# Partial products collected from two PSUM banks at a time, branch gating over all tokens in one step, and one modulation buffer in two merges of a two-layer diffusion backbone

## The chip, the cores and the metric

The kernel runs on one core of a Trainium2 chip as one program. The metric is device time in microseconds, the median of several runs. PE is TensorE, DVE is VectorE, ACT is ScalarE, POOL is GpSimd, and SP is the engine that issues all DMAs here.

## The reference, cut to what matters

Two layers work on 512 latent and 256 context tokens of width 1024. The second layer computes outputs for the latent tokens only.

```python
h = rms_norm(x, g_pre) * (1 + scale) + shift              # scale, shift, gate from silu(c) @ w_mod
z = h @ w_in                                              # 11 pieces of 512 columns, and 3 x 1024 merge logits
o_ret  = rms_norm(retention(rq, rk, rv)) * silu(rg)       # branch r
o_mlp  = mu * (w_s @ layer_norm(mv) + b_s) * silu(mg)     # branch m
o_diff = rms_norm(diff_attention(dq, dk, dv)) * silu(dg)  # branch d
y   = sum over b in r, m, d of sigmoid(logits_b) * (o_b @ w_bo[b])
out = x + gate * rms_norm(y @ w_o, g_post)
```

## The kernel before, in words

**Numbers.** Every large matmul is made of three: weights and activations are split into a high part in fp32r (a copy on ACT, line 341) and a low part (a subtraction on DVE, line 353), and high x high, high x low and low x high are summed in PSUM.

**Blocks.** Weights come as named blocks of 256 output columns. `dl`, `rl`, `ml` are the merge logits of the branches d, r and m, four blocks each; `db`, `rb`, `mb` are the branch output weights, four each; `rg`, `mg`, `mu`, `dg`, `mv` are the gates and inputs of the branches, two each. A block is loaded into `raw[0]` or `raw[1]`, two buffers of 2048 words a partition that take turns, `mg0` into `raw[0]` and `mg1` into `raw[1]`. From there it is split into slots in the fp32r area `AR`.

**Seven products.** Where the table `SEVEN` names a block (`dl`, `rl`, `ml`, `mg`, `mu` in both layers, `rg` in the first), `seven` (line 1581) computes a 2 x 2 block product with seven instead of eight half-size products, after Strassen and Winograd. A product is 12 matmuls over n = 384 tokens in layer 0 and n = 256 in layer 1, into a PSUM bank of its own. It is added to running sums: one copy on ACT, then seven adds on DVE, each of one product. A finished quarter goes to `done`, which takes its sigmoid on ACT, and the like. The weights of a product are one of seven pieces that `p_split` makes, up to five pieces ahead (`NSLOT`); four more DVE instructions form the pieces' sums.

**Merges.** `merge` (line 1705) runs for d, r and m in turn. For each of four blocks it computes the sigmoids of the logits, then the branch products for two groups of 128 channels, span by span (two spans of 384 tokens in layer 0, one of 512 in layer 1). Each span's product is gated by one DVE multiplication and added to `Y`, by POOL in merge r and DVE in merge m.

**Modulation.** While layer 0's merges run, DVE also computes the modulation vectors that are needed later. `mod_begin` (line 1047) sets up buffers of 1024 words in `AF`: n for the rows of `w_mod`, n = 2, and two for the silu of the two conditioning rows. `mod_load` brings in a part of `w_mod` (512 KB), and `mod_item` sums its product with each of the two conditioning rows, one custom DVE instruction each (line 376), whose elementwise result is junk and goes to the upper half of `raw[1]`. That half is free as long as the blocks alternate between 2048 and 1024 words, which they do in a merge. Merge d takes eight such loads, merges r and m twelve each, a few behind each group of channels (`MODS`).

**Order.** The functions only record operations, in program order, with the memory that they read and write. `Rec.schedule` (line 406) then list-schedules them: it steps through time with an estimated cost for each operation and puts on each engine the ready operation of the lowest priority number, which is the program order plus a bump by kind. The result is emitted as one fixed order an engine. So a change in one stage can move instructions in later ones. In the attention stage of a layer (`dr_phase`) units of differential attention (`d_unit`: scores, softmax, transposes, product with V) and of retention are interleaved on PE with projections in groups of 24 matmuls, which take turns in two PSUM banks.

Of the kernel before, what the change touches and what calls it, by code (L numbers as in the profile page):

```python
# [200 lines left out]
class Rec:  # L201
# [14 lines left out]
    def iv(self, ap):  # L216
        pat = ap.ap
        t = ap.tensor
        sp = str(ap.space)
        if "DRAM" in sp.upper() or type(t).__name__ == "DRamTensorHandle":  # L220
            ext = 1 + sum((n - 1) * s for s, n in pat)
            return "D" + t.name, [(ap.offset, ap.offset + ext)], None
        ps = pat[0][0]
        f = ap.offset % ps
        p0 = ap.offset // ps
        outer, ln = [], 1
        dims = [d for d in pat[1:] if d[0] != 0 and d[1] > 1]
        while dims:
            s, n = dims[-1]
            if s == ln or (ln == 1 and s <= 2):  # L230
                ln = (n - 1) * s + ln
                dims.pop()
            else:
                break
        starts = [f]
        for s, n in dims:
            starts = [x + s * k for x in starts for k in range(n)]
        return t.name, [(x, x + ln) for x in starts], range(p0 // 32, (p0 + pat[0][1] - 1) // 32 + 1)
# [346 lines left out]
class Prog:  # L585
# [995 lines left out]
    def seven(self, l, name, done):  # L1581

        R, F = self.R, self.F
        n = self.half(l)
        tag = R.tag = f"L{l}.{name}"
        S1, S2, S3, S4 = (self.SX[j] for j in range(4))

        def p(x, A):
            wh, wl = self.pw[self.ahead(l, name, x)]
            R.tag = tag  # L1590
            ps = self.P(n)
            with R.pe():
# [8 lines left out]
        def add(out, ps, f):
            R.tt(out.ap, ps.ap, f.ap, ALU.add)

        def give(m, t, c):
            done(m, n * t, n * t + n, c.ap)
            c.free()
# [12 lines left out]
        ps.free()
        p5 = p(3, S1)  # L1620
        c12 = F(n)
        add(c12, p5, u)
        ps = p(4, S3)
        add(u, ps, u)
        ps.free()
        c = F(n)
        add(c, p5, u)
        p5.free()
        give(1, 1, c)
        ps = p(5, self.halves(1, 1))  # L1630
        add(u, ps, u)
        ps.free()
        give(0, 1, u)
        ps = p(6, S4)
        add(c12, ps, c12)
        ps.free()
        give(1, 0, c12)
# [67 lines left out]
    def merge(self, l, c, extra=None):  # L1705
# [7 lines left out]
                self.fm.take(o, o + n)  # L1713
                self.Y.append(Buf(self.fm, self.AFl, o, n, (n,)))
        for p in range(4):
            G = {}

            def done(m, a, b, ps):
                if m not in G:
                    G[m] = F(n)  # L1720
# [12 lines left out]
            if SEVEN[l]:  # L1733
                q = self.ahead(l, name)
                W = [[x[:, k] for x in self.pw[q + e]] for e in range(2) for k in range(2)]
            else:
                self.begin(l, name)
                hi, lo = self.W(l, name, 256, 0, 4)
                W = [(hi[:, k], lo[:, k]) for k in range(4)]
            for m in range(2):  # L1740
                i = 2 * p + m
                y = self.Y[i]
                for v, a, b in self.spans(l) if l == 0 or not end else ((0, 0, 256), (1, 256, 512)):
                    R.tag = f"L{l}.{name}"
                    pb = self.P(b - a)
                    with R.pe():
                        for k in range(4):
                            wh, wl = (x[:, 128 * m:128 * m + 128] for x in W[k])
                            xh, xl = (x[:, k, a:b] for x in self.OT)
                            R.mm(pb.ap, wh, xh, k == 0, False)  # L1750
                            R.mm(pb.ap, wh, xl, False, False)
                            R.mm(pb.ap, wl, xh, False, k == 3)
                    R.tag += ".ev"
                    g = G[m][:, a:b]
                    R.tt(y[:, a:b] if first else g, pb.ap, g, ALU.mult)
                    pb.free()
# [274 lines left out]
    def run(self):  # L2031
# [4 lines left out]
        for l in range(DEPTH):  # L2036
# [125 lines left out]
```

## Time and profile before

| | |
|---|---|
| runs | 1476.3, 1476.57, 1474.8 us; median 1476.3 |
| profiled execution | 1477.75 us, of which the span of instructions 1476.0 |
| granted TensorE clock | 0.999 of full speed |
| attention stages | about 63 to 376 us (layer 0), 866 to 1138 (layer 1) |
| merges d, r and m, layer 0 | about 402 to 502, 522 to 625, 679 to 786 |
| gMLP stage (`mg`, `mu`), layer 0; layer 1 | about 614 to 692; 1308 to 1370 |
| DVE instructions | 2119, busy 1086.6 us |

Rows of the profile name line, engine, operation and the tiles that it writes and reads: `AR` is the fp32r area, `AF` the float area, `PSM` is PSUM. `x12` counts instructions; times are us unless marked ns. A `<-` behind an idle time names what ended it.

### The profile page before, as it was taken

The numbers are of one execution on the slowest core, as the hardware profiler recorded it, in microseconds if no ns is written. First come the engines' busy times: TensorE is split into PE (matmuls) and PEld (weight loads), VectorE is DVE, ScalarE is ACT, GpSimd is POOL, SyncE is SP. The second block draws the span as 40 slices with busy tenths as digits, with TensorE's granted clock in tenths as the row PEclk, the third lists the DMA queues.
The fourth block names the chain that finished last, engine by engine and source line by source line (L and its number), as shares of the span: only waits on it lengthen the run. The fifth ranks groups of instructions, "written<-read, shape, count | busy, mean of one in ns | idle before, by whom it ended". The sixth has DMA issues, their size and how long they took to land.

```text
span 1476.0 us, 24501 instructions
## 1 busy us (share of the span) xinstructions
PE 1448.1 (98%) x9424; PEld 1354.4 (92%) x9424; DVE 1086.6 (74%) x2119; ACT 689.6 (47%) x1488; POOL 173.6 (12%) x195
## 2 busy tenths in 40 slices
PE   6999999999999999999999999999999999999998
PEld 4789898999999999999999898989898998999997
DVE  4456655557998799999996645674858786899982
ACT  6735653564343343344346443564455354444551
POOL 1211211211000002211001111111111000111000
PEclk9999999999999999999999999999999999999999
DMA  9351322112223334322364234141212222322332
GB/s 362 124 162 58 88 69 68 37 63 81 91 103 129 108 107 145 127 78 103 120 228 147 73 127 131 63 122 44 86 51 81 70 101 106 129 94 87 142 129 72
DMA packets 38869, 159.00 MB, mean 108 GB/s; under 512 B 5472, under 2 KB 6624, under 8 KB 29280
## 3 DMA queue, kind: packets, MB, share of 16 engines
q1 hardware_dynamic: 38752, 157.43, 31.4%
q8 instruction: 74, 1.21, 0.3%
q14 instruction: 43, 0.35, 0.1%
HBM read 135.39 MB, written 6.82 MB: 96 GB/s over the span
## 4 chain that ended last, share of the span: by engine, by line
PE 83%; DVE 9%; issue 3%; DMA 2%; ACT 2%; POOL 1%; SPq 1%; DVEq 0%; POOLq 0%; ACTq 0%
PE PSM L316 79%; DVE AR L353 3%; DVE AF L353 3%; PE PSM L320 3%; DMA AF<-w 1%; POOL AF L394 1%; ACT AF L341 1%; DVE AF L372 1%; SPq L403 1%; ACT AR L341 1%; DMA AF<-x 0%; DVE AF L362 0%; DVE AF L368 0%; DVE AF L376 0%; DVE AF L360 0%
## 5 line engine op out<-in xcount | busy, mean ns | idle before, releaser
L316 PE MATMUL PSM<-AR 128*128 128x256 f32 (+2 forms) x7896 | 1305.4, 324 | 4.6 <-DVE AF L353 3.9
L316 PEld LDWEIGHTS PSM<-AR 128*128 128x128 f32 x7896 | 1190.8, 190 | 76.6 <-ACT AF L341 3.8
L341 ACT ACTIVATE AR<-AF 128x512 fp32r<-128x512 f32 (+5 forms) x623 | 356.6, 601 | 340.7 <-PE PSM L316 174.6
L353 DVE TENSOR_TENSOR AR<-AF,AR 128x512 fp32r<-128x512 f32 (+4 forms) x620 | 407.5, 681 | 72.3 <-ACT AR L341 67.1
L353 DVE TENSOR_TENSOR AF<-PSM,AF 128x384 f32<-128x384 f32 (+3 forms) x461 | 237.2, 530 | 126.7 <-PE PSM L316 66.9
L394 POOL TENSOR_TENSOR AF<-AF 128x128 f32<-128x128 f32 (+7 forms) x188 | 172.9, 932 | 1297.4 <-DVE AF L353 452.5
L341 ACT ACTIVATE AF<-PSM 128x256 f32<-128x256 f32 (+5 forms) x321 | 137.5, 448 | 201.4 <-PE PSM L316 170.4
L353 DVE TENSOR_TENSOR AF<-AF 128x512 f32<-128x512 f32 (+6 forms) x268 | 160.5, 622 | 15.5 <-PE PSM L316 4.2
L341 ACT ACTIVATE AF<-AF 128x256 f32<-128x256 f32 (+5 forms) x227 | 110.2, 512 | 122.0 <-DVE AF L353 104.4
L316 PE MATMUL PSM<-AF 128*128 128x128 f32 (+3 forms) x1104 | 142.8, 304 | 11.8 <-DMA AF<-wmodn 9.1
L316 PEld LDWEIGHTS PSM<-AF 128*128 128x128 f32 (+1 forms) x1104 | 126.4, 185 | 21.3 <-DVE AF L376 9.1
L341 ACT ACTIVATE AF<-PSM,AF 128x768 f32<-128x768 f32 (+2 forms) x144 | 90.8, 646 | 88.6 <-DVE AF L360 53.1
L372 DVE TENSOR_REDUCE AF<-PSM 128x2 f32<-128x1536 f32 (+1 forms) x40 | 61.6, 1542 | 34.2 <-PE PSM L316 33.9
L362 DVE TENSOR_SCALAR AF<-AF 128x1 f32<-128x1 f32 (+3 forms) x188 | 42.7, 237 | 49.4 <-ACT AF L341 42.9
L320 PE MATMUL PSM<-AF 128*128 128x128 f32 x424 | 68.1, 278 | 5.3 <-ACT AF L341 4.1
L376 DVE CUSTOM_DVE_ANT_0 AF<-AF 128x1024 f32<-128x1024 f32 (+1 forms) x60 | 72.8, 1213 | 0.0
L320 PEld LDWEIGHTS PSM<-AF 128*128 128x128 f32 x424 | 50.8, 142 | 17.3 <-ACT AF L341 7.3
L368 DVE SCALAR_TENSOR_TENSOR AF<-AF 128x768 f32<-128x768 f32 (+2 forms) x48 | 44.2, 928 | 3.6 <-POOL AF L394 2.7
L353 DVE TENSOR_TENSOR AF<-AF,AR 128x512 f32<-128x512 f32 (+2 forms) x40 | 29.8, 766 | 0.6 <-PE PSM L316 0.5
L368 DVE SCALAR_TENSOR_TENSOR AF<-AF,PSM 128x128 f32<-128x128 f32 x64 | 20.5, 344 | 10.8 <-PE PSM L316 5.5
L362 DVE TENSOR_SCALAR AF<-PSM,AF 128x128 f32<-128x128 f32 x48 | 15.8, 402 | 12.7 <-PE PSM L320 12.7
L360 DVE TENSOR_SCALAR AF<-AF 128x2 f32<-128x2 f32 (+5 forms) x98 | 21.4, 235 | 2.1 <-ACT AF L341 0.7
(22 smaller groups left out, 103.9 us busy)
## 6 DMA issues: line engine op xcount, KB each, us to landing
AF<-w SPq DMA_DIRECT2D x74, 1024.0 KB, 4.9
AF<-wmod SPq DMA_DIRECT2D x32, 512.0 KB, 3.5
AF<-w SPq DMA_DIRECT2D x26, 512.0 KB, 4.4
AF<-wmodn SPq DMA_DIRECT2D x16, 512.0 KB, 8.9
AF<-x SPq DMA_DIRECT2D x12, 512.0 KB, 4.3
AR<-AR SPq DMA_DIRECT2D x16, 384.0 KB, 4.2
AF<-AF SPq DMA_DIRECT2D x64, 64.0 KB, 2.0
AF<-const SPq DMA_DIRECT2D x4, 512.0 KB, 3.6
```

Source lines behind the costliest of these rows:

```text
L316: self.add("PE", lambda: pe.matmul(out, lhsT, rhs, start=start, stop=stop), [out], [lhsT, rhs], c)
L320: self.add("PE", lambda: pe.transpose(out, in_, ident), [out], [in_, ident], 109.0)
L341: return self.add("ACT", lambda: e.activation(out, in_, func, **kw), outs, ins, c, tab)
L353: return self.add("DVE", lambda: v.tensor_tensor(out, a, b, op=op), [out], [a, b], self.n(out) / 0.97 + 84)
L360: f = lambda: v.tensor_scalar(out, a, s1, None, op0=op0)
L362: f = lambda: v.tensor_scalar(out, a, s1, s2, op0=op0, op1=op1)
L368: return self.add("DVE", lambda: v.scalar_tensor_tensor(out, a, s, b, op0=op0, op1=op1), [out], ins, self.n(out) / 0.97 + 130)
L372: return self.add("DVE", lambda: v.tensor_reduce(out, in_, axis=AX.X, op=op), [out], [in_], self.n(in_) / 0.96 + 72)
L376: return self.add("DVE", lambda: v.tensor_tensor_reduce(junk, a, b, 1.0, 0.0, ALU.mult, ALU.add, accum), [junk, accum], [a, b], self.n(a) ...
L394: return self.add("POOL", lambda: g.tensor_tensor(out, a, b, op=op), [out], [a, b], c)
L403: return self.add("SP", lambda: e.dma_start(out=out, in_=in_), [out], [in_], 475 if "DRAM" in str(in_.space).upper() else 650, nbytes=nb)
```

## The change

`seven` allocates two banks for a pair of products and adds both with one DVE instruction of 2n elements; the seven adds become four. Banks are released when a pair is done, and the finished quarters are handed on in pairs. In `merge` the branch products of both spans go into one two-bank tile and are gated by one multiplication, followed by one add into `Y`, except in the last block of merge m; the sigmoid buffers are allocated up front. `mod_begin` gets n = 1 for the merges d and r: one buffer for parts of `w_mod`, placed so that the area shrinks by 1024 words. A line in the bookkeeping of intervals treats short accesses with stride two exactly.

```diff
-            if s == ln or (ln == 1 and s <= 2):
+            if s == ln or (ln == 1 and s <= 2 and n > 16):
...
-        self.modb = self.At(7680, n + 2, DM)
+        self.modb = self.At(3584 + 1024 * (n + 2), n + 2, DM)
...
+        def two(x, A, y, B):
+            ps = self.P(2, 512)
+            p(x, A, ps[:, 0, 0:n])
+            p(y, B, ps[:, 1, 0:n])
             return ps
...
-        u = F(n)
-        ps = p(0, self.halves(0, 0))
-        R.copy_a(u.ap, ps.ap)
+        e = F(2, n)
+        u = e[:, 0]
+        ps = self.P(n)
+        p(0, self.halves(0, 0), ps.ap)
+        R.copy_a(u, ps.ap)
         ps.free()
-        c = F(n)
-        ps = p(1, self.halves(0, 1))
-        add(c, ps, u)
+
+        ps = two(1, self.halves(0, 1), 2, S2)
+        d = F(2, n)
+        R.tt(d.ap, ps[:, :, 0:n], u.unsqueeze(1).to_broadcast([128, 2, n]), ALU.add)
         ps.free()
-        give(0, 0, c)
...
+        done(0, 0, n, d[:, 0])
+
+        ps = two(3, S1, 4, S3)
+        R.tt(e.ap, ps[:, :, 0:n], d[:, 1:2].to_broadcast([128, 2, n]), ALU.add)
+        R.tt(d[:, 1], ps[:, 0, 0:n], e[:, 1], ALU.add)
         ps.free()
+        done(1, n, 2 * n, d[:, 1])
+        d.free()
+
+        ps = self.P(2, 512)
+        p(5, self.halves(1, 1), ps[:, 1, 0:n])
+        p(6, S4, ps[:, 0, 0:n])
+        R.tt(e.ap, ps[:, :, 0:n], e.ap, ALU.add)
         ps.free()
+        done(0, n, 2 * n, e[:, 1])
+        done(1, 0, n, e[:, 0])
+        e.free()
...
+                pb = self.P(len(cuts), 512)
+                for v, a, b in cuts:
...
+                            R.mm(pb[:, v, 0:h], wh, xh, k == 0, False)
+                            R.mm(pb[:, v, 0:h], wh, xl, False, False)
+                            R.mm(pb[:, v, 0:h], wl, xh, False, k == 3)
+                R.tag += ".ev"
+
+                for v0, v1 in [(v, v + 1) for v in range(len(cuts))] if end else [(0, len(cuts))]:
+                    cols = slice(h * v0, h * v1)
+                    g = G[m][:, cols]
+                    yc = y[:, cols]
+                    w = lambda x: x.rearrange("p (a b) -> p a b", b=h)
+                    R.tt(w(yc if first else g), pb[:, v0:v1, 0:h], w(g), ALU.mult)
...
-                self.mod_begin()
+                self.mod_begin(1)
             self.merge(l, "d", lambda i: extra(i, MODS[0][i]))
```

**What moves, first place.** SP's order from the end of merge r into the gMLP stage of layer 0. `wmod` is a modulation load, `w 128x2048` and `w 128x1024` are weight blocks. Before, the block of 1024 words is `rb3`, and the `w 128x2048 x2` are `mg0` and `mg1`:

```order
L403 DMA AF<-w 128x1024
L403 DMA AF<-wmod 128x1024 x2
L403 DMA AF<-w 128x2048 x2
L403 DMA AF<-wst 128x512
L403 DMA AF<-bs 128x512
```

In the changed kernel, from `rb3` too; the single `w 128x2048` is `mg0`, and the `x4` are `mu0`, `mg1`, `mu1` and `ml0`:

```order
L403 DMA AF<-w 128x1024
L403 DMA AF<-wmod 128x1024 x2
L403 DMA AF<-wst 128x512
L403 DMA AF<-wmod 128x1024
L403 DMA AF<-w 128x2048
L403 DMA AF<-bs 128x512
L403 DMA AF<-wmod 128x1024 x3
L403 DMA AF<-w 128x2048 x4
```

Three modulation loads and `mu0`'s load have moved ahead of `mg1`'s.

DVE's order at the same place. `L376 ISA AF<-AF 128x1024` is a modulation sum. Before, the two are those over the last load of merge r; the `AR` row behind the first belongs to `rb3`, the one behind the second is `mg0`'s first subtraction:

```order
L376 ISA AF<-AF 128x1024
L376 ISA AF 128x1
L353 TENSOR_TENSOR AR<-AF,AR 128x512
L353 TENSOR_TENSOR AF<-PSM,AF 128x384
L376 ISA AF<-AF 128x1024
L376 ISA AF 128x1
L353 TENSOR_TENSOR AR<-AF,AR 128x512
L353 TENSOR_TENSOR AF<-PSM,AF 128x384
L353 TENSOR_TENSOR AF<-AF 128x4x128
```

In the changed kernel, from the add over the 4th and 5th product of `mg0` (`128x768`); the sum behind it is the last one over the last load of merge r, and the `AR` row is `mg1`'s first subtraction:

```order
L353 TENSOR_TENSOR AF<-PSM,AF 128x768
L376 ISA AF<-AF 128x1024
L376 ISA AF 128x1
L353 TENSOR_TENSOR AF<-PSM,AF 128x384
L353 TENSOR_TENSOR AF<-AF 128x2x2
L360 TENSOR_SCALAR AF<-AF 128x2
L353 TENSOR_TENSOR AF<-AF 128x384
L353 TENSOR_TENSOR AF<-PSM,AF 128x768
L353 TENSOR_TENSOR AF<-AF 128x384 x2
L353 TENSOR_TENSOR AF<-PSM,AF 128x384 x2
L353 TENSOR_TENSOR AR<-AF,AR 128x512 x2
```

The last sum has moved from ahead of `mg0` to behind its 5th product. The two `PSM,AF 128x384` ahead of the `AR` row belong to six matmuls of 128x128 that PE now takes between `mg0`'s seventh product and `mg1`'s first.

**Second place.** PE's order near the end of layer 1's attention stage. `128x512 x2, 128x256 x4, 128x512 x2` are the scores of one attention unit, `L320 x6` its transposes, `L316 AF 128x128 x6` its product with V, and `128x256 x24` a group of projection matmuls. Before, from the scores of the third unit of head 3 (the `x8` holds two transposes of a retention unit and six of the second unit, the `x7` the third unit's six and one more):

```order
L316 MATMUL PSM<-AR 128x512 x2
L316 MATMUL PSM<-AR 128x256 x4
L316 MATMUL PSM<-AR 128x512 x2
L320 MATMUL PSM<-AF 128x128 x8
L316 MATMUL PSM<-AR 128x256 x24
L320 MATMUL PSM<-AF 128x128
L316 MATMUL PSM<-AF 128x128 x6
L316 MATMUL PSM<-AR 128x256 x24
L320 MATMUL PSM<-AF 128x128 x7
```

In the changed kernel, from the same scores to the next projections:

```order
L316 MATMUL PSM<-AR 128x512 x2
L316 MATMUL PSM<-AR 128x256 x4
L316 MATMUL PSM<-AR 128x512 x2
L316 MATMUL PSM<-AF 128x128 x6
L316 MATMUL PSM<-AR 128x512 x2
L316 MATMUL PSM<-AR 128x256 x2
L320 MATMUL PSM<-AF 128x128
L316 MATMUL PSM<-AR 128x256 x2
L316 MATMUL PSM<-AR 128x512 x2
L320 MATMUL PSM<-AF 128x128 x6
L316 MATMUL PSM<-AR 128x256 x24
```

Two groups of projections stood between the third unit's scores and its transposes; now the fourth unit's scores stand there, and the projections come behind. ACT's order there, in the changed kernel: `PSM,AF 128x768` are the third unit's two exponentials, and the `128x256` behind them is the copy that empties the projections' PSUM bank:

```order
L341 ACTIVATE AF<-PSM,AF 128x768
L341 ACTIVATE AF<-PSM,AF 128x128
L341 ACTIVATE AF<-PSM,AF 128x768
L341 ACTIVATE AF<-PSM 128x128
L341 ACTIVATE AF<-PSM 128x256
L341 ACTIVATE AF<-PSM 128x768
```

That copy is the one that the next group of 24 waits for.

More of the change, by code (lines that the diff above doesn't have):

```diff
@@ L1586, in seven, with p @@
         S1, S2, S3, S4 = (self.SX[j] for j in range(4))
-        def p(x, A):
+        def p(x, A, ps):
             wh, wl = self.pw[self.ahead(l, name, x)]
             R.tag = tag
-            ps = self.P(n)
             with R.pe():
@@ L1594, in p @@
                     a, b = A[0][:, k], A[1][:, k]
-                    R.mm(ps.ap, wh[:, k], a, k == 0, False)
-                    R.mm(ps.ap, wh[:, k], b, False, False)
-                    R.mm(ps.ap, wl[:, k], a, False, k == 3)
+                    R.mm(ps, wh[:, k], a, k == 0, False)
+                    R.mm(ps, wh[:, k], b, False, False)
+                    R.mm(ps, wl[:, k], a, False, k == 3)
             R.tag += ".ev"
-            return ps
[L1601 to L1606, printed above, removed]
-        u = F(n)
-        ps = p(0, self.halves(0, 0))
-        R.copy_a(u.ap, ps.ap)
+        def two(x, A, y, B):
+            ps = self.P(2, 512)
+            p(x, A, ps[:, 0, 0:n])
+            p(y, B, ps[:, 1, 0:n])
+            return ps
+        e = F(2, n)
[3 more added lines that the diff above has]
+        R.copy_a(u, ps.ap)
         ps.free()
-        c = F(n)
-        ps = p(1, self.halves(0, 1))
-        add(c, ps, u)
+        ps = two(1, self.halves(0, 1), 2, S2)
+        d = F(2, n)
+        R.tt(d.ap, ps[:, :, 0:n], u.unsqueeze(1).to_broadcast([128, 2, n]), ALU.add)
         ps.free()
-        give(0, 0, c)
-        ps = p(2, S2)
-        add(u, ps, u)
+        done(0, 0, n, d[:, 0])
+        ps = two(3, S1, 4, S3)
+        R.tt(e.ap, ps[:, :, 0:n], d[:, 1:2].to_broadcast([128, 2, n]), ALU.add)
+        R.tt(d[:, 1], ps[:, 0, 0:n], e[:, 1], ALU.add)
         ps.free()
[L1620 to L1624, printed above, removed]
-        ps.free()
[L1626 to L1637, printed above, removed]
+        done(1, n, 2 * n, d[:, 1])
[4 more added lines that the diff above has]
+        R.tt(e.ap, ps[:, :, 0:n], e.ap, ALU.add)
+        ps.free()
+        done(0, n, 2 * n, e[:, 1])
+        done(1, 0, n, e[:, 0])
+        e.free()
     def eight(self, l, name, done):
@@ L1715, in merge @@
         for p in range(4):
-            G = {}
+            G = [F(n), F(n)]
             def done(m, a, b, ps):
-                if m not in G:
-                    G[m] = F(n)
                 R.act(G[m][:, a:b], ps, AF.Sigmoid)
@@ L1742, in merge @@
                 y = self.Y[i]
-                for v, a, b in self.spans(l) if l == 0 or not end else ((0, 0, 256), (1, 256, 512)):
+                cuts = self.spans(l) if l == 0 or not end else ((0, 0, 256), (1, 256, 512))
+                h = cuts[0][2]
+                pb = self.P(len(cuts), 512)
+                for v, a, b in cuts:
                     R.tag = f"L{l}.{name}"
-                    pb = self.P(b - a)
                     with R.pe():
@@ L1749, in merge @@
                             xh, xl = (x[:, k, a:b] for x in self.OT)
[L1750 to L1756, printed above, removed]
+                            R.mm(pb[:, v, 0:h], wh, xh, k == 0, False)
[8 more added lines that the diff above has]
+                    R.tt(w(yc if first else g), pb[:, v0:v1, 0:h], w(g), ALU.mult)
                     if last:
-                        R.tt(y[:, a:b], y[:, a:b], g, ALU.add)
+                        R.tt(yc, yc, g, ALU.add)
                     elif not first:
-                        R.ptt(y[:, a:b], y[:, a:b], g, ALU.add)
+                        R.ptt(yc, yc, g, ALU.add)
+                pb.free()
                 G[m].free()
```

## Prediction

> **What bounds the kernel now.** I read the page's busy shares first, then the list of waits, then PE's timeline, then windows cut at the stages that the change touches.
>
> ```profile
> span 1476.0 us, 24501 instructions
> PE 1448.1 (98%) x9424; PEld 1354.4 (92%) x9424; DVE 1086.6 (74%) x2119; ACT 689.6 (47%) x1488; POOL 173.6 (12%) x195
> PE PSM L316 <- DMA AF<-wmodn: 9.1, 1, 9.1
> PE PSM L316 <- DVE AF L353: 4.2, 7, 1.1
> PE PSM L320 <- ACT AF L341: 4.1, 6, 1.1
> ```
>
> PE (TensorE) works 98% of the span. 9.1 us of its idle time is the first load. All else that it waits for in 1476 us is some 12 us, and only 4.2 us of that is for DVE (VectorE), the engine that the change relieves. So fewer DVE instructions can return only a few us, while each new hole in PE's row is paid in full. Where are the 4.2 us?
>
> ```profile
> 522.00:614.00 92.00, 91.76 (x530) 91.44 (x529) 91.45 (x158) 34.45 (x63) 18.27 (x12) 1.00 0.36 125
> 614.00:680.00 66.00, 66.00 (x399) 66.00 (x398) 62.21 (x109) 27.67 (x49) 12.26 (x8) 1.00 0.23 80
> 1308.00:1338.00 30.00, 30.00 (x238) 29.30 (x237) 29.57 (x55) 14.63 (x31) 3.51 (x3) 1.00 0.24 90
> 1338.00:1368.00 30.00, 26.75 (x216) 25.85 (x216) 30.00 (x61) 13.50 (x28) 5.49 (x4) 1.00 0.28 102
> 1436.00:1476.00 40.00, 33.79 (x175) 28.89 (x174) 11.76 (x26) 5.08 (x16) 2.22 (x4) 0.95 0.20 66
> ```
>
> The columns are the stretch and its length, then busy time of PE, PEld, DVE, ACT and POOL, the granted clock, and DMA. In layer 0's merge r (522 to 614) DVE works 91.45 of 92 us, yet PE loses only 0.24; in its gMLP stage (614 to 680) PE loses nothing. In layer 1's gMLP stage (1308 to 1368) DVE works 59.57 of 60 us and PE idles 3.25. There alone does DVE set the time.
>
> **DVE's saving.** The change removes 130 DVE instructions: 3 in each of 34 seven-product blocks, 28 in layer 0's merges. Element counts stay. DVE in that stage:
>
> ```profile
> 1351.41 0.68 DVE L353 TENSOR_TENSOR AR<-AF,AR 128x512 fp32r<-128x512 f32 x1
> ...
> 1352.02 0.41 DVE L353 TENSOR_TENSOR AF<-AF 128x256 f32<-128x256 f32 x1
> 1352.35 0.41 DVE L353 TENSOR_TENSOR AF<-PSM,AF 128x256 f32<-128x256 f32 x1
> 1352.69 1.35 DVE L353 TENSOR_TENSOR AR<-AF,AR 128x256 fp32r<-128x256 f32 x3
> ```
>
> An add of 512 holds DVE for 0.61 us (1351.41 to 1352.02), one of 256 for 0.33 to 0.34. Two of 256 made one save 0.07, so a block saves 3 x 0.07 = 0.2 us. Four such blocks and the start of a fifth lie in 1308 to 1368: 1.0 us less DVE work where DVE is the bound, so PE's 3.25 us fall by **1.0**. Bounds: 0, if the pairs are collected later by as much, and 3.25, if the new order also spreads the rest; I take 1.0 because no row shows more being removed. [...] Elsewhere PE hides DVE, and the saving is worth 0.2 us at most (layer 0, merge r).
>
> What the pairs add stays hidden. A pair holds two PSUM banks from its first product until its add; with eight banks PE can be three pairs, six products, ahead of an add that takes about 1 us. A merge's product over both token halves comes one branch product later, and its result is read a whole merge later. POOL, 12% busy, makes one add of 768 where it made two of 384. Should a pair be collected so late that PE meets a full PSUM, each such case costs at most one add, 1 us; it is in the bounds of the saving. The line in the interval bookkeeping leaves the order as it was, by itself.
>
> **The single modulation buffer.** This part removes nothing from DVE; it moves work. Each load, the two conditioning rows' as well, has to wait until the previous one is used up.
>
> ```profile
> AF<-w SPq DMA_DIRECT2D x74, 1024.0 KB, 4.9
> AF<-wmod SPq DMA_DIRECT2D x32, 512.0 KB, 3.5
> L376 DVE CUSTOM_DVE_ANT_0 AF<-AF 128x1024 f32<-128x1024 f32 x56 | 71.9, 1284 | 0.0
> L353 DVE TENSOR_TENSOR AF<-PSM,AF 128x256 f32<-128x256 f32 x158 | 64.3, 420 | 48.9 <-ACT AF L341 25.0 <-PE PSM L316 20.0 <-POOL AF L394 1.6
> L353 DVE TENSOR_TENSOR AF<-PSM,AF 128x384 f32<-128x384 f32 x190 | 101.4, 551 | 20.3 <-PE PSM L316 15.0 <-ACT AF L341 4.3
> L353 DVE TENSOR_TENSOR AF<-PSM,AF 128x512 f32<-128x512 f32 x105 | 70.6, 686 | 52.0 <-PE PSM L316 26.4 <-ACT AF L341 19.9 <-POOL AF L394 5.2
> L353 DVE TENSOR_TENSOR AR<-AF,AR 128x512 fp32r<-128x512 f32 x462 | 323.3, 720 | 48.2 <-ACT AR L341 43.9 <-PE PSM L316 2.3
> L341 ACT ACTIVATE AR<-AF 128x512 fp32r<-128x512 f32 x462 | 278.6, 627 | 258.5 <-PE PSM L316 172.6 <-DVE AF L353 44.4 <-DMA AF<-w 33.7
> 671.60 83.45 PE L316 MATMUL PSM<-AR 128*128 128x384 f32 x480
> 651.77 2.84 PE L316 MATMUL PSM<-AF 128*128 128x128 f32 x24
> 654.36 14.81 PE L316 MATMUL PSM<-AR 128*128 128x384 f32 x84
> 609.16 5.93 SPq L403 DMA_DIRECT2D AF<-w  x2
> ```
>
> One turn costs at least 3.5 + 2 x 1.28 = 6.1 us, and merge r asks for two loads in every half pass. The order shows the result: on SP six of merge r's twelve modulation loads now stand behind that merge's last weight load, three of them even behind block mg0's. Their sums write their junk into the upper half of raw[1], and block mg1's weights go to raw[1]; so mg1's load cannot be issued before the last sum. In DVE's order that sum stands behind the add over mg0's 4th and 5th product, and thus behind PE.
>
> Count from mg0's first matmul. A product is 12 matmuls of 83.45/480 = 0.174 us, 2.09 us. The 5th ends at 10.4. The add of 2 x 384 is not in this trace; by 420, 551 and 686 ns for 256, 384 and 512 (1.05 ns an element) it is about 0.95. Then the sum, 1.28; the load, 4.9; ACT's copy 0.63; DVE's subtraction 0.72; and hand-offs of about 0.1 each, 0.5 in all. mg1's first piece is ready at 19.4. PE has mg0's seven products, 14.6, and six small matmuls that the order puts ahead (12 took 654.36 - 651.77 = 2.59), 1.3: it runs dry at 15.9. **PE waits 3.5 us**, where before it waited for nothing. Behind it the next pieces need 0.7 us of DVE each against 2.09 us of PE, so it stays one hole. PE is the bound behind it until 1308, so nothing gives it back. Bounds: 2, if landing takes 3.5 us as for a load half the size; 5.6, if the chain of loads comes late by one product. The cover that it had is gone: with two buffers mg1's load followed mg0's directly, and both were issued by 615.1 (609.16 + 5.93), before mg0's products began (14 products, 29.2 us, ahead of the small matmuls at 651.77: 622.5). SP's later loads queue behind it: only mu1's and ml0's, two blocks ahead of their use.
>
> **The order of layer 1's attention.** The shifted list schedule also moves this stage. Rows of one unit there (head 3, third and fourth block of queries), before:
>
> ```profile
> 1083.65 1.75 DVE L372 TENSOR_REDUCE AF<-PSM 128x2 f32<-128x1536 f32 x1
> ...
> 1086.11 0.90 ACT L341 ACTIVATE AF<-PSM,AF 128x768 f32<-128x768 f32 x1 [0.87 <-DVE AF L360]
> ...
> 1087.01 0.89 ACT L341 ACTIVATE AF<-PSM,AF 128x768 f32<-128x768 f32 x1
> ...
> 1088.53 1.02 DVE L368 SCALAR_TENSOR_TENSOR AF<-AF 128x768 f32<-128x768 f32 x1
> ...
> 1091.12 0.93 PE L320 MATMUL PSM<-AF 128*128 128x128 f32 x7
> ...
> 1091.80 1.65 PE L316 MATMUL PSM<-AR 128*128 128x512 f32 x8
> ...
> 1093.29 1.50 PE L316 MATMUL PSM<-AF 128*128 128x128 f32 x12
> 1093.49 1.76 DVE L372 TENSOR_REDUCE AF<-PSM 128x2 f32<-128x1536 f32 x1 [3.82 <-PE PSM L316]
> 1094.55 3.12 PE L316 MATMUL PSM<-AR 128*128 128x256 f32 x24
> ```
>
> From the scores' last matmul the softmax takes 0.2 us to the maximum, and from 1083.65 to 1089.55, 5.9 us, to the row that lets PE transpose: 6.1 us. In that time PE had groups of 24 projection matmuls of 3 us each. In the new order, between the scores of the third unit and its transposes stand only 6 products with V (1093.29 to 1094.55: 1.26), the fourth unit's scores (1091.80 to 1093.29: 1.49) and one transpose (seven took 1091.12 to 1091.80, so 0.10). The next group of 24 can't be taken earlier: its PSUM bank is emptied by an ACT copy that stands behind this unit's exponentials. **PE waits 6.1 - 2.9 = 3.2 us.** Bounds: 2, if the products with V themselves come late and fill the hole; 5, if the ACT copy or DVE's queue adds.
>
> **The sum** against the profiled execution (1477.75 us, 1.75 of it outside the span): -1.0 - 0.2 + 3.5 + 3.2 = **+5.5 us**. That execution is 1.45 above the median of 1476.3; the forecast for the median is **1481.8 us**. About 0.2%, 3 us, is what a measurement here can tell from no change.
>
> **Rivals.**
> - Only one hole opens. If mg1's load comes early, or the attention order costs nothing since DVE and ACT run ahead, the sum is +2.0 to +2.3: 1478.3 to 1478.6, within 0.2%, or beyond it where the one hole is larger. For it: both holes are priced from an order, not from a wait seen. Against: each rests on a dependence, not on a tight race. 18%.
> - Faster: DVE's bound in layer 1 is the kernel's only repairable wait and goes altogether, 3.25 + 0.2, while the loads chain so fast that mg1's is issued before mg0's 3rd product ends, and ACT copies the bank out in time: 1472.9. It decides whether the last sum really waits for the 5th product; DVE's order says that it does. 7%.
> - The clock falls in the new holes. The window 1436 to 1476 is the only one above with a granted clock below 1.00, 0.95, and the one with PE's longest idleness, 6.2 us; 5% of 40 us is 2 us, lost if it happens ahead of work. Twice, that makes 1485.8. [...] 15%.
> - DVE in layer 0's gMLP stage is overrun: to 62.21 of 66 us come six late sums, 7.7 us, less 0.8 saved; with the 3.5 us hole that makes 69.1 of 69.5, and a further 1 to 2 us of waits: 1483.3. This lies in the forecast's own range.
>
> **How the numbers follow.** The forecast (both holes, no throttling) has 57%, its own range 1479 to 1486. 3% are left for an order that acts elsewhere. Slower by over 0.2%: 55 of the forecast's 57, the clock's 15, some 5 of the one-hole case's 18, 2 of the rest: 0.77. Within: 2 + 13 + 1 = 0.16. Faster: 0.07. The range runs from the one-hole case, 1478.3, to the clock's with a margin for a late chain, 1488.
>
> **What would show it.** In the profile after: DVE with 130 fewer instructions and about 10 us less time held; on PE a wait of 3 to 4 us for DMA, ACT or DVE near 640 us, ahead of mg1, and PE's share of the stretch 614 to 684 below 97%; one or two waits of 3 us in all near 1100; and less than 3.25 us of idleness in layer 1's gMLP stage. The prediction is wrong if mg1's load is issued before mg0's 5th product ends, or if PE's waits outside the first load stay at 12 us.

## The result and the profile after

The changed kernel takes 1491.8 us (median of 4 runs, 1490.4 to 1495.2) against 1476.4 us before: slower by 1.08%, ratio 1.0108 with a 95% interval of 1.0096 to 1.012. The forecast was 1481.8 us, its range ended at 1488.0. So the sign was right, and the forecast loss of 5.4 us is about a third of the 15.3 measured. The profiled execution of after took 1490.4 us, with a span of 1488.5.

The page's first lines of after:

```profile
span 1488.5 us, 24328 instructions
PE 1452.3 (98%) x9424; PEld 1358.6 (91%) x9424; DVE 1079.6 (73%) x1989; ACT 688.4 (46%) x1488; POOL 177.5 (12%) x187
```

Against before the span is 12.5 us longer. PE's idle time (span less busy) went from 27.9 to 36.2 us, +8.3. PE's busy time went from 1448.1 to 1452.3 for the same 9424 matmuls, +4.2: these ran slower. DVE has the 130 instructions fewer that were forecast, and 7.0 us less busy time instead of about 10. In the list of PE's waits (us in total, number, longest) one is new and long:

```profile
PE PSM L316 <- DVE AF L353: 9.7, 5, 6.3
```

The windows of after, cut at the places that the prediction named (columns as before: stretch, length, busy PE, PEld, DVE, ACT and POOL, granted clock, DMA share, GB/s):

```profile
636.00:640.00 4.00, 1.04 (x9) 0.85 (x7) 3.71 (x9) 0.52 (x1) 0.00 (x0) 0.99 0.40 131
640.00:644.00 4.00, 0.61 (x3) 0.61 (x4) 2.59 (x5) 1.41 (x3) 0.00 (x0) 0.50 0.60 238
644.00:648.00 4.00, 3.39 (x12) 2.88 (x12) 2.89 (x5) 1.15 (x3) 0.00 (x0) 0.50 0.01 2
648.00:652.00 4.00, 4.00 (x19) 4.00 (x19) 3.03 (x6) 1.80 (x4) 0.00 (x0) 0.73 0.02 4
1100.00:1104.00 4.00, 3.50 (x27) 3.13 (x25) 2.22 (x3) 1.28 (x4) 0.00 (x0) 1.00 0.00 0
1104.00:1108.00 4.00, 1.64 (x8) 1.32 (x9) 0.95 (x6) 2.75 (x8) 0.55 (x1) 0.95 0.24 90
1108.00:1112.00 4.00, 3.99 (x21) 3.27 (x21) 3.10 (x4) 1.81 (x3) 0.74 (x2) 0.63 0.31 113
1338.00:1350.00 12.00, 10.77 (x92) 10.59 (x91) 12.00 (x24) 6.50 (x16) 1.45 (x1) 1.00 0.25 89
1350.00:1380.00 30.00, 28.12 (x234) 27.77 (x233) 30.00 (x57) 14.32 (x29) 5.89 (x3) 1.00 0.32 108
```

A window's loss is counted as its idle time plus its busy time multiplied by what the clock lacks. That is an estimate; two stretches of after bear it out: 106 matmuls of 128x384 from 617.84 took 18.53 us at a clock of 1.00, 0.175 each, and 12 from 646.28 took 4.12 us, 0.343 each, where the clock was 0.50 up to 650. Ahead of mg1, 636 to 652: idle 2.96 + 3.39 + 0.61 = 7.0, clock 0.61 x 0.50 + 3.39 x 0.50 + 4.00 x 0.27 = 3.1, together **10.1 us**. In layer 1's attention, 1100 to 1112: idle 0.50 + 2.36 + 0.01 = 2.9, clock 1.64 x 0.05 + 3.99 x 0.37 = 1.6, together **4.4 us**. Before, neither place lost anything: PE was busy all of 614 to 680 and of 1080 to 1120, at a clock of 1.00. In after, PE's timeline at the second place shows two waits for the softmax on ACT, one ahead of each half of the fourth unit's scores:

```profile
1105.39 0.97 PE L316 MATMUL PSM<-AR 128*128 128x512 f32 x4 [1.89 <-ACT AF L341]
...
1107.43 1.55 PE L316 MATMUL PSM<-AR 128*128 128x256 f32 x4 [0.97 <-ACT AF L341]
```

The two places make 14.5 us, where the span grew by 12.5; the rest of the kernel got 2 us shorter. Layer 1's gMLP stage gave little of it: PE idles 1.23 + 1.88 = 3.1 us there, against 3.25.

How the hole ahead of mg1 came about is in the timelines of after. First SP, which issues the loads, then ACT and PE:

```profile
623.00 9.16 SPq L403 DMA_DIRECT2D AF<-wmod  x2
632.44 6.44 SPq L403 DMA_DIRECT2D AF<-w  x2
```

```profile
643.52 1.15 ACT L341 ACTIVATE AR<-AF 128x512 fp32r<-128x512 f32 x2 [1.49 <-DMA AF<-w]
```

```profile
636.21 0.83 PE L316 MATMUL PSM<-AF 128*128 128x128 f32 x6
643.39 1.65 PE L316 MATMUL PSM<-AF 128*128 128x128 f32 x6 [6.35 <-DVE AF L353]
644.69 0.99 PE L316 MATMUL PSM<-AR 128*128 128x384 f32 x2
646.28 6.04 PE L316 MATMUL PSM<-AR 128*128 128x384 f32 x23 [0.61 <-DVE AR L353]
```

Then DVE, rows of the same stretch, L376 the modulation sums:

```profile
622.90 1.87 DVE L353 TENSOR_TENSOR AF<-AF 128x4 f32<-128x4 f32 x2
...
625.87 3.53 DVE L353 TENSOR_TENSOR AR<-AF,AR 128x512 fp32r<-128x512 f32 x3
629.32 1.21 DVE L376 CUSTOM_DVE_ANT_0 AF<-AF 128x1024 f32<-128x1024 f32 x1
...
630.58 1.22 DVE L376 CUSTOM_DVE_ANT_0 AF<-AF 128x1024 f32<-128x1024 f32 x1
...
635.28 1.23 DVE L376 CUSTOM_DVE_ANT_0 AF<-AF 128x1024 f32<-128x1024 f32 x1 [0.85 <-DMA AF<-wmod]
...
636.43 0.95 DVE L353 TENSOR_TENSOR AF<-PSM,AF 128x768 f32<-128x768 f32 x1
637.30 1.22 DVE L376 CUSTOM_DVE_ANT_0 AF<-AF 128x1024 f32<-128x1024 f32 x1
...
642.77 0.56 DVE L353 TENSOR_TENSOR AF<-PSM,AF 128x384 f32<-128x384 f32 x1
645.07 0.56 DVE L353 TENSOR_TENSOR AF<-PSM,AF 128x384 f32<-128x384 f32 x1 [1.74 <-PE PSM L316]
645.55 1.28 DVE L353 TENSOR_TENSOR AR<-AF,AR 128x512 fp32r<-128x512 f32 x2
```

Read backwards. mg1's first two matmuls run at 644.69. The third waits until 646.28 for DVE's subtraction (645.55), which stands in DVE's order behind an add (645.07) over the second half of the small matmuls. The program has six of these; each leaves two records, so an `x6` is three of them. The second half started only at 643.39, when DVE's add over the first half (642.77) had ended. So the wait of 6.35 us itself ended with DVE's own backlog. mg1's load came at almost the same time: ACT began to copy its pieces at 643.52, and one of the two copies takes 0.6.

Both go back to the last modulation sum, which ended at 637.30 + 1.22 = 638.5. SP issued mg1's load right behind it, last of two, at about 638.6 (632.44 + 6.44 less the 0.3 of an issue). DVE collected the rest of mg0 and added over the small matmuls only behind it. That sum follows the add over mg0's 4th and 5th product (636.43), as the order of the changed kernel says, and DVE came to that add only when the sum ahead of it was done, which had waited for its own load until 635.28. This load, the last one for the modulation, had been issued at about 631.8 (623.00 + 9.16 less 0.3), right after the sums of the load before it (630.58 + 1.22 = 631.8). Those sums had started at 629.32 though their load was issued at 623.0; DVE was late, and two entries ahead of them are far too long: 1.87 us for two adds of four elements, 3.53 for three subtractions. The rows of POOL lie beside both:

```profile
621.91 2.76 POOL L394 TENSOR_TENSOR AF<-AF 128x768 f32<-128x768 f32 x1 [18.31 <-DVE AF L353]
626.03 2.22 POOL L394 TENSOR_TENSOR AF<-AF 128x768 f32<-128x768 f32 x1 [1.35 <-DVE AF L353]
```

### The profile page after: what moved, and what is told of

The parts are those of the page before. It is cut to its first block, busy times and chain, and to the rows that moved or that the text cites. A ratio compares the mean times of both kernels' runs of the same rounds, so it can differ in the third digit from the quotient of the medians.

```text
span 1488.5 us, 24328 instructions
## 1 busy us (share of the span) xinstructions
PE 1452.3 (98%) x9424; PEld 1358.6 (91%) x9424; DVE 1079.6 (73%) x1989; ACT 688.4 (46%) x1488; POOL 177.5 (12%) x187
## 4 chain that ended last, share of the span: by engine, by line
PE 50%; DVE 3%; DMA 1%; issue 1%; ACT 1%; POOL 0%; DVEq 0%; POOLq 0%; ACTq 0%
PE PSM L316 49%; PE PSM L320 1%; DVE AR L353 1%; DMA AF<-w 1%; DVE AF L353 1%; ACT AR L341 0%; ACT AF L341 0%; POOL AF L394 0%; DVE AF L362 0%; DVEq L2158 0%; DVE AF L360 0%; POOLq L2158 0%; ACTq L341 0%; DVE AF L368 0%
## 5 line engine op out<-in xcount | busy, mean ns | idle before, releaser
L316 PE MATMUL PSM<-AR 128*128 128x256 f32 (+2 forms) x7896 | 1309.6, 325 | 8.8 <-DVE AF L353 3.1
L316 PEld LDWEIGHTS PSM<-AR 128*128 128x128 f32 x7896 | 1193.2, 190 | 80.6 <-ACT AF L341 4.9
L341 ACT ACTIVATE AR<-AF 128x512 fp32r<-128x512 f32 (+3 forms) x623 | 356.4, 602 | 340.6 <-PE PSM L316 171.4
L353 DVE TENSOR_TENSOR AR<-AF,AR 128x512 fp32r<-128x512 f32 (+4 forms) x620 | 412.1, 690 | 89.5 <-ACT AR L341 85.6
L394 POOL TENSOR_TENSOR AF<-AF 128x128 f32<-128x128 f32 (+6 forms) x180 | 176.8, 992 | 1306.1 <-DVE AF L362 486.3
L353 DVE TENSOR_TENSOR AF<-PSM,AF 128x512 f32<-128x512 f32 (+4 forms) x337 | 221.8, 668 | 121.2 <-PE PSM L316 61.5
L316 PE MATMUL PSM<-AF 128*128 128x128 f32 (+3 forms) x1104 | 143.7, 305 | 17.9 <-DMA AF<-wmodn 9.0
L316 PEld LDWEIGHTS PSM<-AF 128*128 128x128 f32 (+1 forms) x1104 | 127.4, 185 | 27.9 <-issue 9.8
L341 ACT ACTIVATE AF<-PSM,AF 128x128 f32<-128x128 f32 (+2 forms) x144 | 90.8, 646 | 82.0 <-DVE AF L360 53.1
L376 DVE CUSTOM_DVE_ANT_0 AF<-AF 128x1024 f32<-128x1024 f32 (+1 forms) x60 | 68.9, 1149 | 6.1 <-DMA AF<-wmod 5.8
L320 PE MATMUL PSM<-AF 128*128 128x128 f32 x424 | 68.8, 279 | 3.4 <-ACT AF L341 3.3
L320 PEld LDWEIGHTS PSM<-AF 128*128 128x128 f32 x424 | 51.6, 143 | 15.0 <-ACT AF L341 5.8
L360 DVE TENSOR_SCALAR AF<-AF 128x2 f32<-128x2 f32 (+4 forms) x98 | 20.2, 222 | 3.2 <-PE PSM L320 1.0
```

The costliest lines, as they stand in the source:

```text
L316: self.add("PE", lambda: pe.matmul(out, lhsT, rhs, start=start, stop=stop), [out], [lhsT, rhs], c)
L320: self.add("PE", lambda: pe.transpose(out, in_, ident), [out], [in_, ident], 109.0)
L341: return self.add("ACT", lambda: e.activation(out, in_, func, **kw), outs, ins, c, tab)
L353: return self.add("DVE", lambda: v.tensor_tensor(out, a, b, op=op), [out], [a, b], self.n(out) / 0.97 + 84)
L360: f = lambda: v.tensor_scalar(out, a, s1, None, op0=op0)
L376: return self.add("DVE", lambda: v.tensor_tensor_reduce(junk, a, b, 1.0, 0.0, ALU.mult, ALU.add, accum), [junk, accum], [a, b], self.n(a) ...
```

## The experiments

The theory after this reading: the single buffer's late loads make the hole ahead of mg1; GpSimd's adds lengthen the chain that leads to it; the clock makes both holes dearer; the attention order makes the second hole. The rivals: the pairs and the gating over both halves cost the time themselves; the holes are a place where any wait shows, and would move elsewhere.

| | kernel | median us | ratio to before, 95% interval |
|---|---|---|---|
| 1 | after, modulation loads earlier | 1480.8 | 1.0029 (1.0018 to 1.004) |
| 2 | after, attention order | 1486.7 | 1.0067 (1.0048 to 1.0085) |
| 3 | before with one buffer | 1497.5 | 1.0138 (1.0123 to 1.0153) |
| 4 | after without merge r's adds on POOL | 1483.8 | 1.0047 (1.0031 to 1.0064) |
| 5 | after with both repairs | 1474.8 | 0.999 (0.9981 to 0.9999) |
| 6 | after with filler matmuls | 1493.4 | 1.0121 (1.0106 to 1.0136) |
| 7 | before with the gating alone | 1480.7 | 1.0027 (1.0017 to 1.0037) |
| 8 | 7 without merge r's adds on POOL | 1475.7 | 0.9989 (0.998 to 0.9998) |
| 9 | 7 with modulation loads earlier | 1479.1 | 1.0017 (1.0008 to 1.0026) |
| 10 | 5 with single adds | 1487.4 | 1.0075 (1.0061 to 1.0089) |

**1. The loads earlier.** Only the table of modulation loads is changed; the sum over the merges stays.

```diff
-MODS = [2, 1, 1, 2, 1, 1, 0, 0], [2, 2, 2, 2, 2, 2, 0, 0], [2, 2, 2, 2, 2, 2, 0, 0]
+MODS = [2, 2, 1, 2, 2, 1, 0, 0], [2, 2, 2, 2, 2, 0, 0, 0], [2, 2, 2, 2, 2, 2, 0, 0]
```

> The kernel after, with two of merge r's twelve modulation loads given to merge d (ten and ten instead of eight and twelve). In the order the last modulation load then stands ahead of block mg1's, and mg1's load ahead of mu0's. Theory (late loads): the loss of 10.3 us in 625 to 650 goes, since mg1's weights no longer wait for a sum that stands behind mg0's products: 1481.5 us (1480 to 1483.5), and PE waits less than 1 us between 630 and 650. Rival (the pairs and the gating over both halves cost it themselves, by PSUM held longer or DVE late): the loads hardly matter, 1489 to 1492, and a wait of 4 us or more stays in mg0 or mg1.

Measured 1480.8 us, 11.0 less than after. The windows of this kernel where after lost 10.1 us:

```profile
636.00:640.00 4.00, 4.00 (x25) 4.00 (x24) 3.97 (x7) 1.22 (x3) 0.00 (x0) 1.00 0.00 0
640.00:644.00 4.00, 4.00 (x25) 4.00 (x24) 3.75 (x7) 2.88 (x6) 0.00 (x0) 1.00 0.01 4
```

No idle time and the full clock. Pairs, gating and the single buffer are all still there, so none of them costs anything at this place once the last modulation sum and mg1's load are early. The theory holds.

**2. The order of layer 1's attention.** The priority of the attention units is shifted in layer 1 alone:

```diff
-        self.R.bump = ABUMP
+        self.R.bump = -60 if self.layer else ABUMP
```

> The kernel after, with the bump of layer 1's attention units set from -100 to -60; the order then has groups of 24 projection matmuls between the scores of head 3's third unit and its transposes again. Nothing else changes place before layer 1. Theory: the waits near 1103 to 1109 (3.6 us) and the lower clock behind them (1.5 us) go, 1486.8 us (1485.5 to 1488.5). Rival (DVE and ACT are the limit there, so the wait shows up elsewhere in the stage): 1490 to 1492.5.

Measured 1486.7 us, 5.0 less than after. The two windows with the wait and the low clock are full now:

```profile
1104.00:1108.00 4.00, 4.00 (x33) 3.66 (x32) 3.38 (x5) 3.33 (x10) 1.39 (x3) 1.00 0.54 199
1108.00:1112.00 4.00, 4.00 (x37) 4.00 (x36) 1.82 (x5) 3.20 (x11) 0.55 (x1) 1.00 0.02 4
```

**3. One buffer alone.** The kernel before, with two lines of the change:

```diff
-        self.modb = self.At(7680, n + 2, DM)
+        self.modb = self.At(3584 + 1024 * (n + 2), n + 2, DM)
...
-                self.mod_begin()
+                self.mod_begin(1)
```

> The kernel before with one modulation buffer in merges d and r, and nothing else of the change: seven single adds, gating span by span. In its order four modulation loads stand behind mg0's load on SP and two of them behind mu0's too. Theory (the single buffer makes the hole): slower than before by about as much as the whole change, or more, since one more turn of the buffer (9 us in the trace of after) lies ahead of mg1's load: +16 us, 1492 (1488 to 1497), with one long PE wait ahead of mg1. Rival (the hole needs the pairs): 1476 to 1479.

Measured 1497.5 us, 20.7 more than before on the same chip: the sign and the mechanism of the theory, a little beyond its range. On SP and PE of this kernel:

```profile
645.22 14.03 SPq L403 DMA_DIRECT2D AF<-w  x2
```

```profile
639.67 0.94 PE L316 MATMUL PSM<-AF 128*128 128x128 f32 x6 [3.54 <-DVE AF L353]
650.76 11.55 PE L316 MATMUL PSM<-AR 128*128 128x384 f32 x54 [10.16 <-ACT AR L341]
```

mg1's load leaves 6.6 us later than in after, and PE waits 3.5 and 10.2 us. So the single buffer by itself is worse than the whole change; with the other two parts it is milder, and which of them does that was not run.

**4. No adds on POOL.** In merge r the add into `Y` is left out:

```diff
-                    elif not first:
-                        R.ptt(yc, yc, g, ALU.add)
```

> The kernel after without GpSimd's 16 adds into Y in merge r (8 of 768 and 8 of 512), so branch r is missing from its sum; every other engine keeps its order but for two places of DVE. Theory (DVE instructions that run beside such an add are stretched, by 1.65 us beside one of 768 and 1.1 beside one of 512, and two of these lie in the chain ahead of mg1): DVE's busy time falls from 1079.6 by about 20 us to 1058 to 1062, and the wait ahead of mg1 gets about 3 us shorter: 1487.5 (1486 to 1489.5). Rival (the long DVE instructions have another cause, such as DMA writes): DVE busy stays within 3 us of 1079.6, time 1490.5 to 1492.5.

Measured 1483.8 us, 8.0 less than after; the theory had named 4.3, and the time lies below its range. DVE's busy time falls by 16.0, less than the 20 expected. The page, and DVE's rows that answer to 622.90 and 625.87 of after:

```profile
PE 1448.2 (98%) x9424; PEld 1356.6 (92%) x9424; DVE 1063.6 (72%) x1989; ACT 691.2 (47%) x1488; POOL 146.1 (10%) x171
```

```profile
619.95 0.29 DVE L353 TENSOR_TENSOR AF<-AF 128x4 f32<-128x4 f32 x2
...
621.30 1.28 DVE L353 TENSOR_TENSOR AR<-AF,AR 128x512 fp32r<-128x512 f32 x2
622.99 0.69 DVE L353 TENSOR_TENSOR AR<-AF,AR 128x512 fp32r<-128x512 f32 x1 [0.40 <-ACT AR L341]
623.60 1.22 DVE L376 CUSTOM_DVE_ANT_0 AF<-AF 128x1024 f32<-128x1024 f32 x1
```

The same instructions take 0.29 instead of 1.87 and 1.97 instead of 3.53 us: 3.1 us less. The sum behind them starts at 623.60 instead of 629.32. About half of these 5.7 us lie here, the others earlier in merge r. PE's waits ahead of mg1, and the window with the low clock:

```profile
638.20 0.94 PE L316 MATMUL PSM<-AF 128*128 128x128 f32 x6 [2.65 <-DVE AF L353]
...
640.38 11.85 PE L316 MATMUL PSM<-AR 128*128 128x384 f32 x59 [0.89 <-DVE AR L353]
```

```profile
640.00:644.00 4.00, 3.62 (x13) 3.62 (x14) 3.96 (x7) 1.49 (x3) 0.00 (x0) 0.58 0.01 2
```

Idle 2.65 + 0.89 = 3.5, clock 3.62 x 0.42 = 1.5, in all 5.1 instead of 10.1. So POOL's adds stretch DVE, and half of the hole is their work. The other 3 us lie elsewhere; layer 1's merge r has such adds too, and in the gMLP stage behind it PE idles 1.1 us (1308 to 1380) instead of 3.1. The kernel before has the same adds in halves; there they meet no chain that PE waits for.

**5. Both repairs.** The edits of 1 and 2 together.

> The kernel after with both repairs: ten modulation loads each in merges d and r, and the bump of layer 1's attention units at -60. Theory: the two losses are independent, so the gains add: 1491.8 - 11.0 - 5.0 = 1475.8 us (1474 to 1478), as fast as the kernel before or 1 us faster, since PE's extra time outside the two places was some 2.5 us less in after than in before. Rival (a hole closed in one place opens in another): 1479 to 1481, no better than with the earlier loads alone.

Measured 1474.8 us (11 runs), as the theory said: 17.0 us less than after, where the single gains add up to 16.0. Neither hole opened again, though smaller waits are new: 0.99 us near 628 and 1.71 near 1427. PE's idle time is 27.7 us, against 27.9 before. This is the one kernel here with the reference's whole work that beats the kernel before, by 0.1% (0.01 to 0.19%). The page:

```profile
span 1473.1 us, 24340 instructions
PE 1445.4 (98%) x9424; PEld 1354.0 (92%) x9424; DVE 1076.8 (73%) x1989; ACT 687.3 (47%) x1488; POOL 176.4 (12%) x187
```

**6. Filler ahead of mg1.** Behind mg0's product in layer 0:

```diff
+            if l == 0 and i == 0:
+                R.tag = "fill"
+                ps = self.P(384)
+                for _ in range(8):
+                    with R.pe():
+                        for _ in range(4):
+                            R.mm(ps.ap, self.SX[0][0][:, 0, 0:128], self.SX[0][0][:, 1], True, True)
+                ps.free()
```

> The kernel after with 32 more matmuls of 128x384 (5.6 us by the 0.174 us of one) behind mg0's last product in layer 0, whose result nobody reads. mg1's load is issued as before, so they fill a hole that is there anyway. They also stand ahead of the six small matmuls, so that DVE's subtraction for mg1 no longer waits behind the adds over those. Theory (the hole costs more than its length, since PE runs at half clock behind it): about 2.5 us of half clock goes, and mg1 starts near 644.4 instead of 646.3 with 1.3 us of small matmuls still to do: 1488.2 us (1486.5 to 1489.5), granted clock 1.00 from 640 to 652. Rival (the low clock in the records costs nothing or isn't caused by the idle time): 1490.5 to 1492.5. If mg1's load comes later than 644, the filler costs: above 1492.5.

Measured 1493.4 us: the expected gain didn't come in the total. In the stage itself it did:

```profile
640.00:644.00 4.00, 2.48 (x15) 2.16 (x13) 2.32 (x4) 1.15 (x3) 0.00 (x0) 1.00 0.65 256
644.00:648.00 4.00, 3.42 (x18) 3.10 (x19) 3.51 (x6) 2.47 (x5) 0.00 (x0) 1.00 0.02 6
```

```profile
644.47 7.76 PE L316 MATMUL PSM<-AR 128*128 128x384 f32 x41 [1.99 <-ACT AR L341]
```

mg1 starts at 644.47, as expected, and runs on at the full clock. The stage loses 1.52 + 0.58 idle and 32 x 0.174 = 5.6 for the filler, 7.7 in all instead of 10.1. So in this trace keeping PE busy does save the clock's 3.1 us. But the total is 1.6 us above after, and the span 1.2 (1489.7); so 3.6 us went elsewhere, and they lie in no one place of the trace. On the total the experiment decides nothing: its four runs spread from 1491.3 to 1495.4 us, those of after from 1490.4 to 1495.2.

**7. The gating alone.** The kernel before with the change's `merge` and interval line; single adds, two buffers. Of the edit:

```diff
+                pb = self.P(len(cuts), 512)
...
-                    pb = self.P(b - a)
...
-                    R.tt(y[:, a:b] if first else g, pb.ap, g, ALU.mult)
...
+                    R.tt(w(yc if first else g), pb[:, v0:v1, 0:h], w(g), ALU.mult)
```

> The kernel before with only the merges changed: both spans' branch products in one two-bank tile, one multiplication and one add into Y of 768 elements; two modulation buffers and single adds in the seven-product blocks. mg1's load stands two rows behind mg0's in its order, with every modulation load ahead. Theory (this part costs nothing where the loads are early): 1477.5 us (1476 to 1479). Rival (the gating over both halves, with its 768-element adds on GpSimd, makes the modulation sums late by itself): 1480 or more, with a PE wait near 640.

Measured 1480.7 us: the rival's time. But the wait isn't at 640; it is inside merge r, for block rb3's weights:

```profile
522.00:614.00 92.00, 90.11 (x515) 88.78 (x515) 91.46 (x148) 31.80 (x60) 14.30 (x6) 1.00 0.33 114
```

```profile
607.75 10.52 PE L316 MATMUL PSM<-AR 128*128 128x384 f32 x58 [1.28 <-DVE AR L353]
```

PE idles 1.9 us there, with DVE full (91.46 of 92). The profiled execution, 1477.1 us, is the shortest of this kernel's runs; the rest of the 4 us isn't seen in it.

**8. The gating without adds on POOL.** The edit of 4 in kernel 7.

> The kernel with the gating alone (two modulation buffers, single adds), without GpSimd's 16 adds into Y in merge r, so branch r is missing from its sum; the order of PE and SP is the same row by row. There DVE works 91.46 of the 92 us of merge r, and PE waits 1.3 us for block rb3's weights. Theory (the gating costs its 4 us since DVE is full in merge r, and the 768-element adds on GpSimd stretch it): DVE's busy time in 522 to 614 falls by some 8 to 12 us, PE's wait near 606 goes, 1476.5 us (1475 to 1478). Rival (the cost is that both halves share a two-bank tile, so results are read later): 1479.5 to 1482.

Measured 1475.7 us, 5.0 less than 7. PE's wait near 606 is gone and its idle time in merge r is 0.6:

```profile
522.00:614.00 92.00, 91.37 (x526) 90.74 (x525) 90.17 (x165) 36.51 (x66) 0.00 (x0) 1.00 0.40 139
```

DVE's busy time did not fall by 8 us as expected; in the same 92 us it did 165 instructions instead of 148. It is still full, but ahead. The two-bank tile is still there and costs nothing that shows. In kernel 7 DVE is busy for 1089.2 us, 2.6 more than before with 28 instructions fewer; here for 1074.5. So the price of the gating is in all likelihood that POOL's longer adds hold DVE more. The kernel before without its adds, in halves, was not run; how much of the 5.0 us they would return there is open.

**9. The gating with the loads earlier.** The table of 1 in kernel 7.

> The kernel with the gating alone, with ten modulation loads each in merges d and r instead of eight and twelve: 5.1 us of DVE work (two loads of two sums of 1.28 us) leave merge r, where DVE is full, for merge d, where it is not (82.78 of 100 us). The order of PE is the same row by row. Theory (DVE is full in merge r): the wait near 606 goes, 1477 us (1475.5 to 1478.5). Rival (the two-bank tile itself costs): 1479.5 to 1482. A third way: the sums make merge d late instead, with a PE wait before 502.

Measured 1479.1 us, between the two expectations: 1.7 less than 7. The merge still has DVE full:

```profile
522.00:614.00 92.00, 90.63 (x517) 89.13 (x517) 91.39 (x152) 33.62 (x63) 14.29 (x6) 1.00 0.32 109
```

Taking 5 us of sums away leaves DVE as full as it was, with PE idle 1.4 us instead of 1.9. What 7 loses beyond that stays open.

**10. The repaired kernel with single adds.** Kernel 5 with `seven` of before. Of the edit:

```diff
-        ps = two(1, self.halves(0, 1), 2, S2)
-        d = F(2, n)
-        R.tt(d.ap, ps[:, :, 0:n], u.unsqueeze(1).to_broadcast([128, 2, n]), ALU.add)
+        c = F(n)
+        ps = p(1, self.halves(0, 1))
+        add(c, ps, u)
```

> The kernel with both repairs (1474.8 us), with the seven single adds of before in place of the pairs; gating over both halves, one modulation buffer, ten and ten loads and the bump of -60 stay. Theory: the pairs return about what the prediction's term said, 0.6 to 1.2 us, most of it in 1308 to 1380, where DVE is the bound: 1476 us (1475 to 1477.5). Rival (the pairs cost or bring nothing, and the gain over before has another source): 1473.5 to 1474.8. In its order two modulation loads stand behind mg0's load again, ahead of mg1's; if that opens the hole ahead of mg1, it is above 1478.

Measured 1487.4 us, 12.6 more than 5: a miss of both. No hole opened ahead of mg1 either. The waits lie elsewhere, the longest in merge m:

```profile
708.67 13.62 PE L316 MATMUL PSM<-AR 128*128 128x384 f32 x68 [1.93 <-DVE AF L353]
```

PE waits for DVE's adds in 11 places, 7.1 us in all, against 4 places and 3.2 us in kernel 5. This kernel has 102 more adds (34 blocks with 3 each), and without the pairs its whole order is another one. The experiment changes both at once and doesn't show which of them costs the time. The one stage where DVE sets the time can be compared, layer 1's gMLP; first this kernel, then kernel 5:

```profile
1308.00:1380.00 72.00, 68.71 (x542) 66.63 (x541) 69.52 (x135) 33.25 (x68) 10.27 (x7) 1.00 0.32 110
```

```profile
1308.00:1380.00 72.00, 69.09 (x553) 67.62 (x553) 70.72 (x124) 35.85 (x73) 10.32 (x6) 1.00 0.28 98
```

PE idles 3.3 us with single adds and 2.9 with pairs: 0.4 us for the pairs in this stage.

## Why the prediction was wrong

- **The direction, and the two holes: right.** Both are where the prediction put them, and experiments 1 and 2 remove them one by one. That all else PE waits for is some 12 us also held: it left nothing large to win.
- **The hole ahead of mg1: 3.5 us forecast, 10.1 measured (7.0 idle and 3.1 clock). The mechanism was right, the size wrong, and this is the step that failed.** The prediction counted from the end of mg0's 5th product as if DVE were free then: its add, one sum, the load. mg0's seven products ended where the small matmuls begin, at 636.21, so by 2.09 us a product the 5th ended at 632.0. Its add took the estimated 0.95 us, but it started at 636.43, 4.4 us later, since in DVE's order a sum stands ahead of it that waited for its own load until 635.28. What ended last was the chain of loads: last sums of one load, next load, its sums. By the count the last sum would have ended at 632.0 + 0.95 + 1.28 and two hand-offs, near 634.4; it ended at 638.5, 4.1 late. The landing took its 4.9 us (638.6 to 643.5).
- **"5.6, if the chain of loads comes late by one product" was no upper bound.** It allowed 2.1 us, and nothing in the text bounded how late DVE could be when the first sums of that chain were due.
- **DVE's order cost another 1.4 us.** The first copy ended at 643.52 + 0.6 = 644.1, yet the subtraction came at 645.55. The prediction counted the six small matmuls as work that PE does before it runs dry. Only three of them were. The other three had to wait 6.35 us for DVE's add over the first, and the add over them stands ahead of mg1's subtraction on DVE.
- **The clock: a rival with 15% and 2 us a hole.** It fell in both, for 3.1 and 1.6 us. In experiment 6 the first of these is gone from the stage, though the total did not fall. It belonged into the price of a hole of several us, not beside it as a rival.
- **POOL "makes one add of 768 where it made two of 384": taken as free, and it was not.** Experiments 4 and 8 show that these adds delay DVE. They are no new work of the change, but with the single buffer they lie in the chain that PE waits for. They make 5.0 of the 10.1 us.
- **The attention order: +3.2 forecast, 2.9 idle and 1.6 clock measured**, 5.0 by removing it. PE waited ahead of the two halves of the fourth unit's scores, and not ahead of the third unit's transposes as the prediction had it; the softmax that it waits for is the same. Which part of the change moves this order is open: the single buffer alone (3) and the gating alone (7) leave PE busy for 39.9 and 39.6 of the 40 us from 1080 to 1120, and the pairs alone were not run.
- **DVE's saving: -1.0 forecast, -0.1 to -0.4 measured** in layer 1's gMLP stage (3.25 to 3.1 us idle; 3.3 to 2.9 between kernels 10 and 5). That a saving on a full engine shortens the stage one for one was wrong. What the pairs are worth in the whole kernel is not shown (experiment 10).
- **What stays open.** The medians differ by 15.3 us, the spans of the two traces by 12.5. For after the traced execution is the shortest of its runs, for before it is longer than the four that the ratio uses. What varies between runs of one kernel (experiment 1: 1478.3 to 1485.1) is not settled.

## What to carry to other kernels

When a change takes a buffer from a ring, follow the whole chain of loads, users and reloads to the first thing that was loaded freely before, and ask what that chain writes on its way: here a junk result stood in front of the weights. Price it from the engine that is full at that moment and not from the undisturbed durations. Then look for the cheap repair before judging the change: a table that asks for two loads earlier and a priority for one stage turned 1.08% slower into 0.1% faster.

## What the runs showed of the hardware

**DVE instructions took longer beside an add on POOL.** Two adds of four elements, 0.29 us in experiment 4 where POOL has no such add, took 1.87 beside a POOL add of 768 from 621.91 to 624.67; DVE ended them at 624.77, 0.1 us behind POOL's. Three subtractions took 3.53 instead of 1.97 beside the next. Without these adds (experiment 4) DVE's busy time is 16.0 us lower. What holds DVE beside them no run shows.

**The granted clock fell behind short waits too.** In the wait of 6.35 us it fell to 0.50, stayed there for two windows of 4 us and was 0.73 in a third. After the waits of 1.89 and 0.97 us near 1105 it was 0.63 (1108 to 1112). In experiment 10 the 68 matmuls behind the wait of 1.93 us, which had one of 0.38 us ahead of it, took 13.62 us, 0.200 each, against 0.176 in the 287 from 599.82 (50.49 us). After one wait of 1.99 us (experiment 6) the clock stayed at 1.00. So it fell behind two waits of under 2 us in after and not behind one in experiment 6. The low clock behind the long wait took in over 6 us of PE's work: PE is busy for 6.0 of the 7 us from 643 to 650, at 0.50. From what length of wait on the clock falls these runs don't show.
